# Attention value products half a chunk earlier, the convolution norm's two statistics matmuls one chunk earlier

## The chip, the core and the metric

The kernel runs on one core of one Trainium2 chip. The metric is the device time of one execution in microseconds, the lower the better. Before the change the median of three runs is 650.92 us (650.64 to 651.39).

## What is computed

Two layers of a decoder trunk over 256 positions of 1024 channels. Each layer multiplies its input by one wide matrix (nine blocks of 1024 columns), runs a convolution branch and an attention branch on the results, gates both, merges them and normalizes. Cut to what matters here:

```python
def conformer_conv(a_val, a_glu, conv_w, conv_b, cln_g, cln_b, w_pw2):
    h = a_val * jax.nn.sigmoid(a_glu)
    h = lax.conv_general_dilated(h, conv_w[:, None, :], ...) + conv_b   # depthwise, 31 taps
    h = jax.nn.silu(layer_norm(h, cln_g, cln_b))
    return h @ w_pw2

def hybrid_layer(x, ...):
    u = x @ w_in + b_in
    a_val, a_glu, a_z, q, k, v, b_z, g_a, g_b = jnp.split(u, SPLIT_POINTS, axis=-1)
    h_a = conformer_conv(a_val, a_glu, ...) * jax.nn.silu(a_z)
    y_a = h_a @ w_proj_a
    o = moba_attention(rope(q), rope(k), v)      # 16 heads of 64; causal softmax over 256 positions here
    y_b = (o * jax.nn.silu(b_z)) @ w_proj_b
    merged = jax.nn.sigmoid(g_a) * y_a + jax.nn.sigmoid(g_b) * y_b
    return layer_norm(DEEPNORM_ALPHA * x + merged @ w_out, ln_g, ln_b)
```

## The kernel before

**Chunks.** Every weight matrix is cut into blocks of 256 columns. A block is loaded as float32 (`raw`), and ScalarE (ACT) copies it to a rounded part `hi` in four pieces (L120) while GpSimd (POOL) subtracts to get the rest, `lo` (L124). `gemm_a` (L154) multiplies one block in two chunks, c = 0 and 1, of 128 output channels each. A chunk is 16 matmuls on TensorE (PE): seven `hi` matmuls of 512 columns (L176), eight `lo` matmuls of 256 (L174), and a last `hi`. Its result `mm` lies in one of three PSUM buffers; ACT copies the low half out (`lw`, L182 or L184) and VectorE (DVE) adds it to the high half (L187).

**The stages of a layer.** Value rows first, then the blocks of `A_GLU`, `A_VAL` and `B_Z`, then the 32 chunks of `MID` (Q, K, G_A for each j, then G_B) with the attention between them, then the 8 chunks of `A_Z`, the 8 of `PB` (attention's projection), the 8 of `PW2` (the convolution's), `PA` and `WO`. The convolution's 31 taps run on DVE (L381) in the background until the end of `MID`.

**The attention between chunks.** Eight pairs of heads a layer. A table, `plan`, says after which chunk, or in the middle of which, a pair's three steps are written: `hook(c - 0.5)` is called in a chunk after its eighth matmul, `hook(c)` at its end. `L1`, `L2`, `L3` are the distances in chunks from the pair's K chunk:

```python
at = 2 * n + 1
for p in (2 * j, 2 * j + 1):
    for d, f in ((L1, att_scores), (L2, att_trans), (L3, att_av)):
        plan.setdefault(at + d, []).append((f, p))
    at += 3
```

`att_scores` writes the scores (PE L451), mask and two maxima (DVE L457 to L459), exponentials (ACT L461 twice, L464 twice, each followed by the read of its sum), the reciprocal (DVE L466) and the scaled probabilities `p` (ACT L468, L469, twice). `att_trans` writes six transposes of `p` into two PSUM tiles, `ta` and `tb` (PE L477 to L479), and copies them out as `pa` and `pb` (ACT L482, L483). `att_av` writes the products with the values into the free half of `tb` (PE L491, L494), gates them there (DVE L496) and splits them (ACT L497, DVE L498). The pool of `ta` and `tb` has two buffers, so the `tb` of a pair waits until L498 of the pair before has read its own. Pairs are three chunks apart, and a pair's transposes stand in the same chunk as the scores of the next pair.

**The convolution's norm.** `cln_mu` is the mean's matmul (PE L542) with subtraction and squares, called at the end of `A_Z` chunk `CM`; `cln_var` is the variance's matmul (PE L551) with the chain to the reciprocal root, called after `PB` chunk `CV`; `CB` says after which `PB` chunk each of the eight `cln_b` stands, which write the two halves of `hc` that `PW2` multiplies.

**What sets the order.** On PE the order inside one block of weights is as written; the next block's matmuls may be put between. On ACT and DVE a scheduler decides when the program is built: the order of each engine's instructions is fixed then, and each engine runs its own in that order.

Of the kernel before, what the change touches and what calls it, by code (L numbers as in the profile page):

```python
# [31 lines left out]
NEG = -1e30  # L32
EARLY = 6
NH2 = 2
CM = 5.0
CV = 1
CB = [[], [], [0, 1], [2, 3], [4, 5], [6, 7], [], []]
KE = 7
KN = 5
L1, L2, L3 = 2.5, 5.5, 7.0  # L40
MAN = ''
WARM = 34
NA = 4
# [27 lines left out]
def decoder_trunk(ctx: ExitStack, tc: tile.TileContext, a, out):  # L71
# [19 lines left out]
    def u_pair(name):  # L91

        both = pair.tile([P, KT, 2, S], F32R, tag="p", name=name)
        return both[:, :, 0, :], both[:, :, 1, :], both
# [51 lines left out]
    def background(n):  # L146
        with tc.high_priority(offset=-LATE):
            for _ in range(min(n, len(conv_ops))):
                conv_ops.pop(0)()
# [153 lines left out]
    for l in range(DEPTH):  # L303
# [244 lines left out]
        def cln_var():  # L548
            f = fold(cln["sq"], cln["sq"])
            vp = cvp.tile([P, 2, S], F32, tag="cv", name=f"cvar{l}")  # L550
            nc.tensor.matmul(vp[:, 0, :], ones, f, start=True, stop=True)  # L551
            u = tmp.tile([P, S], F32, tag="g", bufs=2, name=f"cu{l}")
            y = vp[:, 1, :]
            nc.scalar.activation(u, vp[:, 0, :], AF.Sqrt, bias=eps)
            nc.vector.reciprocal(y, u)
            nc.scalar.activation(u, y, AF.Square)
            nc.vector.tensor_scalar(vp[:, 0, :], vp[:, 0, :], EPS, None, op0=ALU.add)
            nc.vector.scalar_tensor_tensor(u, u, -0.5, vp[:, 0, :], op0=ALU.mult, op1=ALU.mult)
            nc.vector.scalar_tensor_tensor(y, u, 1.5, y, op0=ALU.add, op1=ALU.mult)
            cln["r"] = y  # L560

        def cln_b(ct):
            z = ptp.tile([P, 512], F32, tag="pt", name=f"z{l}_{ct}")[:, :S]
            nc.vector.tensor_tensor(z, cv[:, ct, :], cln["r"], op=ALU.mult)
            nc.scalar.activation(z, z, AF.Silu, bias=pc[:, C_LB + ct : C_LB + ct + 1],  # L565
                                 scale=pc[:, C_LG + ct : C_LG + ct + 1])
            nc.scalar.activation(hc[0][:, ct, :], z, AF.Copy)
            nc.vector.tensor_tensor(hc[1][:, ct, :], z, hc[0][:, ct, :].bitcast(F32), op=ALU.subtract)

        def ev_pb(ct, o):  # L570
            nc.vector.scalar_tensor_tensor(gb[:, ct, :], gb[:, ct, :], 1.0, o, op0=ALU.add, op1=ALU.mult)  # L571
            if ct == CV:
                hc.extend(u_pair(f"hc{l}"))
                cln_var()
            for q in CB[ct]:
                cln_b(q)

        def hook_az(c, j):
            if 2 * j + c == CM:
                background(len(conv_ops))  # L580
                cln_mu()
# [178 lines left out]
```

## Time and profile before

| | us |
|---|---|
| median of three runs | 650.92 |
| the profiled execution, its own time | 650.96 |
| its span, first to last instruction | 649.2 |
| PE busy in the span | 634.4 |
| DVE busy | 486.2 |
| ACT busy | 437.7 |
| POOL busy | 486.2 |

The span leaves 1.76 us of the execution's own time outside. Busy times of PE are modelled ends of pipelined matmuls, so distances from start to start say more than durations.

### The profile page before, as it was taken

To read this page: it belongs to the slowest core of one execution; us is meant where nothing else is said; L and a number is where in the kernel's file an instruction comes from. 1 tells how busy PE (TensorE), PEld (TensorE's weight loads), DVE (VectorE), ACT (ScalarE), POOL (GpSimd) and SP (SyncE) were. 2 spreads that over 40 slices of the span, in tenths; PEclk is the share of its full clock that TensorE was granted. 3 is DMA by queue.
4 is the path that set the end of the run, shared out by engine and by line. 5 is a ranking of instruction groups with operands and counts; after the bars stand their busy time and mean duration, and the time that the engine had idled before them with its cause. 6 is when DMAs were issued, how large, how long until landed. Compare 5 with 4: busy or idle time off the path is not lost.

```text
span 649.2 us, 10602 instructions
## 1 busy us (share of the span) xinstructions
PE 634.4 (98%) x3662; PEld 542.3 (84%) x3662; DVE 486.2 (75%) x1130; ACT 437.7 (67%) x1017; POOL 486.2 (75%) x385
## 2 busy tenths in 40 slices
PE   8999999999999999999999999999999999999995
PEld 6888888887878888988788888888877888889884
DVE  4668989999998666455840999899999886664556
ACT  4775665887778689656527566668777787885640
POOL 0089999777566898989628999996677589999850
PEclk9999999999999999999999999999999999999999
DMA  8975555444333564554653555554433344555401
GB/s 268 349 276 211 194 196 195 159 166 131 131 129 131 195 250 152 201 184 187 259 195 113 212 195 199 192 193 152 174 131 130 130 147 178 195 190 186 174 36 65
DMA packets 19190, 116.06 MB, mean 179 GB/s; under 512 B 2112, under 2 KB 3392, under 8 KB 6208
## 3 DMA queue, kind: packets, MB, share of 16 engines
q1 hardware_dynamic: 18560, 114.85, 48.9%
q8 instruction: 29, 0.48, 0.3%
q10 hardware_dynamic: 576, 0.52, 0.3%
q14 instruction: 25, 0.20, 0.1%
HBM read 114.32 MB, written 1.05 MB: 178 GB/s over the span
## 4 chain that ended last, share of the span: by engine, by line
PE 85%; ACT 7%; DVE 4%; DMA 2%; POOL 1%; issue 1%; ACTq 0%; DVEq 0%
PE mm L176 43%; PE mm L174 23%; PE wo L210 3%; PE v L210 3%; PE v L340 3%; ACT hi L120 3%; PE s L451 2%; PE mm L171 2%; DMA raw<-w 2%; PE tb L491 1%; POOL lo L124 1%; ACT z L565 1%; PE tb L479 1%; PE v L331 1%; PE wps L248 1%
## 5 line engine op out<-in xcount | busy, mean ns | idle before, releaser
L124 POOL TENSOR_TENSOR lo<-raw,hi 128x512 fp32r<-128x512 f32 x380 | 485.8, 1315 | 138.7 <-ACT hi L120 134.2
L176 PE MATMUL mm<-x,hi 128*128 128x512 f32 x1024 | 263.8, 395 | 0.0
L120 ACT ACTIVATE hi<-raw 128x512 fp32r<-128x512 f32 x412 | 235.7, 630 | 21.9 <-DMA raw<-w 15.8
L176 PEld LDWEIGHTS mm<-x,hi 128*128 128x128 f32 x1024 | 183.9, 189 | 34.6 <-issue 2.4
L381 DVE SCALAR_TENSOR_TENSOR cv<-h,pc,cv 128x256 f32<-128x256 f32 x464 | 196.4, 481 | 0.2
L174 PEld LDWEIGHTS mm<-x,lo 128*128 128x128 f32 x1024 | 139.4, 190 | 11.3
L174 PE MATMUL mm<-x,lo 128*128 128x256 f32 x1024 | 147.5, 284 | 0.0
L187 DVE TENSOR_TENSOR mm<-mm,lw 128x256 f32<-128x256 f32 x172 | 73.5, 430 | 81.1 <-ACT lw L182 52.1
L182 ACT ACTIVATE lw<-mm,pc 128x256 f32<-128x256 f32 x128 | 61.4, 480 | 88.3 <-PE mm L176 87.9
L176 PE MATMUL mm<-og,hi 128*128 128x512 f32 x128 | 33.1, 395 | 0.0
L210 PE MATMUL wo<-hi,mg 128*128 128x512 f32 (+1 forms) x144 | 32.6, 367 | 0.2 <-DVE mg L610 0.2
L176 PE MATMUL mm<-ah,hi 128*128 128x512 f32 x128 | 32.4, 392 | 0.0
L124 DVE TENSOR_TENSOR lo<-raw,hi 128x512 fp32r<-128x512 f32 x32 | 25.5, 840 | 6.8 <-ACT hi L120 6.7
L210 PEld LDWEIGHTS wo<-hi,mg 128*128 128x128 f32 x144 | 25.2, 189 | 5.3 <-DVE mg L610 0.9
L184 ACT ACTIVATE lw<-mm 128x256 f32<-128x256 f32 x44 | 16.8, 386 | 16.7 <-PE mm L176 15.8
L176 PEld LDWEIGHTS mm<-og,hi 128*128 128x128 f32 x128 | 23.3, 189 | 4.1
L176 PEld LDWEIGHTS mm<-ah,hi 128*128 128x128 f32 x128 | 23.0, 189 | 4.0
L176 PE MATMUL mm<-hc,hi 128*128 128x512 f32 x96 | 25.1, 396 | 0.5 <-DVE gb L571 0.5
L176 PEld LDWEIGHTS mm<-hc,hi 128*128 128x128 f32 x96 | 17.2, 189 | 4.7 <-ACT z L565 1.3
L174 PEld LDWEIGHTS mm<-og,lo 128*128 128x128 f32 x128 | 17.5, 190 | 1.2
L174 PEld LDWEIGHTS mm<-ah,lo 128*128 128x128 f32 x128 | 17.5, 190 | 1.2
L461 ACT ACTIVATE s<-s,nm 128x256 f32<-128x256 f32 x32 | 14.1, 441 | 5.9 <-DVE nm L459 5.9
(134 smaller groups left out, 710.4 us busy)
## 6 DMA issues: line engine op xcount, KB each, us to landing
raw<-w SPq DMA_DIRECT2D x101, 1024.0 KB, 4.8
raw<-w SPq DMA_DIRECT2D x8, 256.0 KB, 5.2
rows<-pr SPq DMA_DIRECT2D x4, 512.0 KB, 6.2
raw<-w SPq DMA_DIRECT2D x2, 512.0 KB, 7.8
xs<-x SPq DMA_DIRECT2D x1, 1024.0 KB, 7.0
out<-xs SPq DMA_DIRECT2D x3, 256.0 KB, 2.0
xf<-xT ACTq DMA_DIRECT2D x4, 128.0 KB, 5.7
xf<-xT SPq DMA_DIRECT2D x2, 256.0 KB, 4.4
```

The source lines that it names most:

```text
L120: nc.scalar.activation(hi[:, ks, :], raw[:, ks, :], AF.Copy)
L124: eng.tensor_tensor(lo[:, ks, :], raw[:, ks, :], hi[:, ks, :].bitcast(F32), op=ALU.subtract)
L171: nc.tensor.matmul(ps[:, 0, :], (wl if q == 2 else wh)[:, k, cs], both[:, k, int(q == 1), :], start=(n == 0), stop=(n == len(seq) - 1))
L174: nc.tensor.matmul(ps[:, 0, :], wl[:, k, cs], both[:, k, 0, :], start=False, stop=False)
L176: nc.tensor.matmul(ps, wh[:, k, cs], both[:, k, :, :], start=(n == 0), stop=(k == KT - 1))
L182: nc.scalar.activation(t, low, AF.Identity, bias=pcs[0][:, b * KT + ct : b * KT + ct + 1])
L184: nc.scalar.activation(t, low, AF.Copy)
L187: nc.vector.tensor_tensor(kept[:, c if b in (Q, K) else 0, :], o, t, op=ALU.add)
L210: nc.tensor.matmul(o, (xl if q == 1 else xh)[:, kk, ts], (wl if q == 2 else wh)[:, k, cols], start=(kk == 0 and n == 0), stop=(kh == 1 and ...
L340: nc.tensor.matmul(o[t], (xl if r == 1 else xh)[:, kk, ts], (wl if r == 2 else wh)[:, k, :], start=(kk == 0 and r == 0), stop=(kk == 7 and ...
L381: r = nc.vector.scalar_tensor_tensor(dst, src, w, acc[:, c, :], op0=ALU.mult, op1=ALU.add)
L461: nc.scalar.activation(s1[:, e, :], s1[:, e, :], AF.Exp, bias=nm[:, 2 + e : 3 + e], accum_out=sm[:, 2 + e : 3 + e])
```

## The change

Four constants differ. `L3` goes from 7.0 to 6.5: the value products of a pair come one chunk after its transposes in place of one and a half, so they stand in the middle of a chunk (after its eighth matmul) and no longer at its end. `CM` goes from 5 to 4 and `CV` from 1 to 0: the two statistics' matmuls stand one chunk earlier. `CB` moves the eight `cln_b` up by one chunk with them. Nothing is added or removed.

```diff
-CM = 5.0
-CV = 1
-CB = [[], [], [0, 1], [2, 3], [4, 5], [6, 7], [], []]
+CM = 4.0
+CV = 0
+CB = [[], [0, 1], [2, 3], [4, 5], [6, 7], [], [], []]
 KE = 7
 KN = 5
-L1, L2, L3 = 2.5, 5.5, 7.0
+L1, L2, L3 = 2.5, 5.5, 6.5
```

The first place is PE's order in layer 0 around the value products of pair 3 (`tb_3`; `mm_1_1959` is the chunk that they stand at), as a difference:

```order
 L176 MATMUL mm_1_1959<-x_94,hi_1712 128x512 x7
-L174 MATMUL mm_1_1959<-x_94,lo_1713 128x256 x8
-L176 MATMUL mm_1_1959<-x_94,hi_1712 128x512
+L174 MATMUL mm_1_1959<-x_94,lo_1713 128x256
 L491 MATMUL tb_3_1911<-pa_3_1918,v_183 64x256 x2
 L494 MATMUL tb_3_1911<-pb_3_1919,v_183 64x128 x2
+L174 MATMUL mm_1_1959<-x_94,lo_1713 128x256 x7
+L176 MATMUL mm_1_1959<-x_94,hi_1712 128x512
```

Seven `lo` matmuls and one `hi` that stood ahead of the products now stand behind them; the other pairs move alike.

The second place is ACT's order in layer 0 around the softmax of pair 5 (`s0_5`, `p0_0_5` and `p1_0_5`); `lw28_0` and `lw28_1` are the copies out of chunks `mm28_0` and `mm28_1`, `tb0_4` is pair 4's. Before:

```order
L461 ACTIVATE s0_5_2057,sm0_5_2063<-s0_5_2057,nm0_5_2062 128x256
L182 ACTIVATE lw28_0_2133<-mm28_0_2116,pc0_181 128x256
L464 ACTIVATE s0_5_2057,sm0_5_2063<-s0_5_2057,nm0_5_2062 128x128 x2
L468 ACTIVATE p0_0_5_2066<-s0_5_2057,rc0_5_2064 128x128
L469 ACTIVATE p1_0_5_2065<-s0_5_2057,rc0_5_2064 128x256
```

And with the change, from `lw28_0` on:

```order
L182 ACTIVATE lw28_0_2140<-mm28_0_2116,pc0_181 128x256
L461 ACTIVATE s0_5_2057,sm0_5_2063<-s0_5_2057,nm0_5_2062 128x256
L182 ACTIVATE lw28_1_2165<-mm28_1_2148,pc0_181 128x256
L461 ACTIVATE s0_5_2057,sm0_5_2063<-s0_5_2057,nm0_5_2062 128x256
L120 ACTIVATE hi30_2178<-raw30_2104 128x512
L464 ACTIVATE s0_5_2057,sm0_5_2063<-s0_5_2057,nm0_5_2062 128x128
L497 ACTIVATE og0_1120<-tb0_4_2046 128x256
L464 ACTIVATE s0_5_2057,sm0_5_2063<-s0_5_2057,nm0_5_2062 128x128
L502 ACTIVATE ga0_1118<-mm28_0_2116 128x256
L120 ACTIVATE hi30_2178<-raw30_2104 128x512
L468 ACTIVATE p0_0_5_2066<-s0_5_2057,rc0_5_2064 128x128
L469 ACTIVATE p1_0_5_2065<-s0_5_2057,rc0_5_2064 128x256
```

The second exponential of pair 5 stood ahead of both copies out and now stands behind both; a copy L497 of pair 4, a gate L502 and two weight pieces L120 have come in ahead of `p`.

The third place is ACT's order around the softmax of pair 4 (`s_4`, `p_0_4`), where `lw_1` is the copy out of the chunk `mm_1_1959` of the first place. Before:

```order
L461 ACTIVATE s_4_1922,sm_4_1928<-s_4_1922,nm_4_1927 128x256
L182 ACTIVATE lw_1_1976<-mm_1_1959,pc_181 128x256
L461 ACTIVATE s_4_1922,sm_4_1928<-s_4_1922,nm_4_1927 128x256
L120 ACTIVATE hi_2002<-raw_1889 128x512
L464 ACTIVATE s_4_1922,sm_4_1928<-s_4_1922,nm_4_1927 128x128
L120 ACTIVATE hi_2002<-raw_1889 128x512
L464 ACTIVATE s_4_1922,sm_4_1928<-s_4_1922,nm_4_1927 128x128
L120 ACTIVATE hi_2002<-raw_1889 128x512 x2
L468 ACTIVATE p_0_4_1931<-s_4_1922,rc_4_1929 128x128
```

And with the change:

```order
L182 ACTIVATE lw_1_1983<-mm_1_1959,pc_181 128x256
L120 ACTIVATE hi_2002<-raw_1889 128x512
L461 ACTIVATE s_4_1922,sm_4_1928<-s_4_1922,nm_4_1927 128x256
L497 ACTIVATE og_1120<-tb_3_1911 128x256
L461 ACTIVATE s_4_1922,sm_4_1928<-s_4_1922,nm_4_1927 128x256
L120 ACTIVATE hi_2002<-raw_1889 128x512
L464 ACTIVATE s_4_1922,sm_4_1928<-s_4_1922,nm_4_1927 128x128
L120 ACTIVATE hi_2002<-raw_1889 128x512
L464 ACTIVATE s_4_1922,sm_4_1928<-s_4_1922,nm_4_1927 128x128
L120 ACTIVATE hi_2002<-raw_1889 128x512
L468 ACTIVATE p_0_4_1931<-s_4_1922,rc_4_1929 128x128
```

The first exponential has gone behind the copy out, and L497 of pair 3, which stood behind `p`, has come between the two. Layer 1 has the same orders at all three places.

## Rows read from the trace of the kernel before

**Rows 1.** The page, busy us by engine (share of the span), instructions

```profile
PE 634.4 (98%) x3662; PEld 542.3 (84%) x3662; DVE 486.2 (75%) x1130; ACT 437.7 (67%) x1017; POOL 486.2 (75%) x385
```

**Rows 2.** Stretch of layer 0's attention: length, busy by engine (instructions), clock, DMA

```profile
113.00:214.00 101.00, 99.43 (x619) 82.41 (x619) 93.00 (x227) 79.74 (x221) 70.72 (x57) 1.00 0.41 144
```

**Rows 3.** Waits of PE: for whom, us in total, times, longest

```profile
PE tb L479 <- DVE og L498: 3.1, 4, 0.8
```

**Rows 4.** Timeline of PE, transposes of pair 5: start, us, what [idle before]

```profile
179.26 2.00 PE L176 MATMUL mm<-x,hi 128*128 128x512 f32 x8
...
181.22 0.27 PE L477 MATMUL ta<-ident,p 128*128 128x128 f32 x1
181.33 0.27 PE L478 MATMUL ta<-ident,p 128*128 128x128 f32 x1
182.40 0.30 PE L479 MATMUL tb<-ident,p 128*128 128x128 f32 x1 [0.79 <-DVE og L498]
```

**Rows 5.** Timeline of DVE, pair 5's maxima and rotation, pair 4's split

```profile
174.07 0.43 DVE L187 TENSOR_TENSOR mm<-mm,lw 128x256 f32<-128x256 f32 x1
...
177.56 0.48 DVE L381 SCALAR_TENSOR_TENSOR cv<-h,pc,cv 128x256 f32<-128x256 f32 x1
...
181.84 0.41 DVE L498 TENSOR_TENSOR og<-tb,og 128x256 fp32r<-128x256 f32 x1
```

**Rows 6.** Timeline of PE, a chunk behind scores and one behind value products

```profile
160.65 1.10 PE L174 MATMUL mm<-x,lo 128*128 128x256 f32 x7
161.59 2.00 PE L176 MATMUL mm<-x,hi 128*128 128x512 f32 x8
...
164.38 0.39 PE L176 MATMUL mm<-x,hi 128*128 128x512 f32 x1
...
165.50 1.88 PE L176 MATMUL mm<-x,hi 128*128 128x512 f32 x7
167.22 1.12 PE L174 MATMUL mm<-x,lo 128*128 128x256 f32 x8
```

**Rows 7.** Timeline of ACT, softmax of pair 4 and start of pair 5's `p`

```profile
162.02 0.48 ACT L182 ACTIVATE lw<-mm,pc 128x256 f32<-128x256 f32 x1 [1.32 <-PE mm L176]
...
164.87 0.47 ACT L182 ACTIVATE lw<-mm,pc 128x256 f32<-128x256 f32 x1 [0.33 <-PE mm L176]
165.24 0.44 ACT L461 ACTIVATE s<-s,nm 128x256 f32<-128x256 f32 x1
...
165.69 0.63 ACT L120 ACTIVATE hi<-raw 128x512 fp32r<-128x512 f32 x1
166.21 0.34 ACT L464 ACTIVATE s<-s,nm 128x128 f32<-128x128 f32 x1
...
166.55 0.64 ACT L120 ACTIVATE hi<-raw 128x512 fp32r<-128x512 f32 x1
...
168.46 0.38 ACT L468 ACTIVATE p<-s,rc 128x128 f32<-128x128 f32 x1
168.71 0.49 ACT L469 ACTIVATE p<-s,rc 128x256 f32<-128x256 f32 x1
...
169.67 0.42 ACT L497 ACTIVATE og<-tb 128x256 fp32r<-128x256 f32 x1
169.93 0.52 ACT L182 ACTIVATE lw<-mm,pc 128x256 f32<-128x256 f32 x1
...
178.47 0.37 ACT L468 ACTIVATE p<-s,rc 128x128 f32<-128x128 f32 x1 [0.24 <-DVE rc L466]
```

**Rows 8.** Timeline of ACT, pair 0's last `p`

```profile
124.88 0.50 ACT L469 ACTIVATE p<-s,rc 128x256 f32<-128x256 f32 x1
```

**Rows 9.** Timeline of PE, the transpose that reads it

```profile
125.47 0.29 PE L478 MATMUL ta<-ident,p 128*128 128x128 f32 x1
```

**Rows 10.** Timeline of PE, first two PW2 chunks of layer 0

```profile
255.44 1.54 PE L176 MATMUL mm<-hc,hi 128*128 128x512 f32 x6
...
261.41 2.00 PE L176 MATMUL mm<-hc,hi 128*128 128x512 f32 x8
```

## Prediction

> **What bounds the kernel now.** I read the page's busy times first. PE is busy 98% of the span, VectorE and GpSimd 75%, ScalarE 67% [rows 1]; only PE's own stops, or more work on PE, can change the time much. The table of stretches shows the same where the change acts: of the 101.00 us of layer 0's attention PE is busy 99.43, at a granted clock of 1.00, which is the 2.4 GHz level [rows 2]. So I looked for PE's waits. One kind lies in the attention: a transpose into `tb` that waits for the split L498, four times, 3.1 us in total [rows 3]. The timeline shows what one costs: pair 5's second transpose starts at 181.33, the third not until 182.40, with seven `lo` matmuls behind it that need nothing new [rows 4]. L498 of pair 4 runs from 181.84 to 182.25 [rows 5] and releases it. The loss is the distance less a normal spacing: 1.07 - (181.33 - 181.22) = 0.96 us.
>
> PE's measure elsewhere: a plain chunk lasts 164.38 - 161.59 = 2.79 us [rows 6]. From the start of a chunk's last `hi` to transposes in the middle of the next chunk it is 181.22 - 179.26 = 1.96 us [rows 4], which are eight `hi` and one `lo`. The other seven `lo` are thus 2.79 - 1.96 = 0.83, one `lo` 0.12, one `hi` 0.23.
>
> **What goes away.** First, the four waits for `tb`. The value products move ahead by seven `lo` and a `hi`, 0.83 + 0.23 = 1.06 us, and the scheduler puts L496 to L498 earlier on their engines too: in ACT's new order pair 4's L497 stands ahead of pair 5's `p`, so that bank is read before the transposes can start at all. 4 x 0.96 = 3.84 us. Second, the norm. `PW2` is the only stage that waits for it: its first two chunks take 261.41 - 255.44 = 5.97 us [rows 10] in place of 5.58. With the statistics and `hc` one chunk, 2.79 us, earlier, the 0.39 goes, once a layer: 0.78. The two statistics matmuls cost PE the same at any chunk's end. Their vector work hides behind the `A_Z` and `PB` chunks, where nothing on PE waits for it; without that cover the 0.39 would only stay. Together 4.62 us gone.
>
> **What the moved products cost on PE.** They now interrupt a chunk in the middle. The nearest rows: after scores in mid-chunk the seven `lo` take 161.59 - 160.65 = 0.94 in place of 0.83, so coming back costs 0.11; after value products at a chunk's end the seven `hi` take 167.22 - 165.50 = 1.72 in place of 1.61, 0.11 as well [rows 6]. I take no difference. The bounds are 0.11 less and 0.11 more for each of the 16: 1.76 us either way.
>
> **What is late next.** Moving the products moves L497 and, with it, the order of ACT. ACT works its list in order, so one instruction that waits holds all behind it. I walk ACT's new list from the rows of the old one, by distances from start to start [rows 7]: L182 165.24 - 164.87 = 0.37; L461 with its sum read 0.45; L120 0.52; L464 with its sum read 0.34; L468 0.25; L497 0.26; L469 (169.67 - 168.46)/2 - 0.25 = 0.35. L502, a copy of the same size, is taken as L497. The walk of the old list checks it: from 164.87, with one L182, one L461, two L464 and four L120, comes 168.45, and L468 stands at 168.46. L182 starts 0.43 us after the start of its chunk's last `hi` (161.59 to 162.02) [rows 6, 7]. A transpose starts 0.09 us after the `p` it reads is done (124.88 + 0.50 to 125.47) [rows 8, 9].
>
> *Pair 5.* Today its `p` starts at 178.47 [rows 7] and the transposes at 181.22 [rows 4], with 2.3 us to spare. In the new order its second L461 stands behind the copy out of `mm28_1`, the chunk just ahead of the one that holds the transposes. Count from the start of that chunk's last `hi`: L182 at 0.43; then L182, L461, L120, L464, L497, L464, L502, L120 come to 0.37 + 0.45 + 0.52 + 0.34 + 0.26 + 0.34 + 0.26 + 0.52 = 3.06, so L468 starts at 3.49 and is done at 3.87. The first transpose starts at 3.96; PE is there at 1.96. The second needs L469: 3.74 + 0.49 + 0.09 = 4.32, the third 4.43. The fourth needs the second L468: 4.09 + 0.38 + 0.09 = 4.56; the fifth the second L469: 4.34 + 0.58 = 4.92; the sixth ends its slot at 5.14. Unhindered it would be 1.96 + 6 x 0.11 = 2.62. The loss is 2.52 us. It hangs only on PE's chunk end, so PE can't run away from it. The first L461 must be done by then too, and it waits for L459, which DVE now takes behind the rotation. Counted from the last `hi` two chunks ahead: L182 at 0.43, L187 some 0.5 later, from it to the tap behind the rotation 3.49 (177.56 - 174.07) [rows 5], L461 0.45, together 4.9; the copy out of `mm28_1` stands two chunks on, at 5.58 + 0.43 = 6.0. That leaves 1.1 us for the large maximum L458, which now falls in between.
>
> *Pair 4.* Its L461 now starts behind L182 and one L120, with L497 between. From the last `hi` of `mm_1_1959`: L182 at 0.43; then L182, L120, L461, L497, L461, L120, L464, L120, L464, L120 are 0.37 + 4 x 0.52 + 2 x 0.45 + 0.26 + 2 x 0.34 = 4.29, so L468 starts at 4.72. Transposes could start at 2.79 + 1.96 = 4.75; they start at 4.72 + 0.38 + 0.09 = 5.19, the second at 4.97 + 0.58 = 5.55, the third at 5.66, the fourth at 5.32 + 0.47 = 5.79. Two `hi` of the next block follow (0.46), then the last two, ready, end at 6.58 in place of 4.75 + 0.66 + 0.46 = 5.87. The loss is 0.71 us.
>
> The other six pairs' `p` keep clear of their transposes by the same walk, pair 6 barely.
>
> **The sum.** Twice a layer's 2.52 + 0.71 is +6.46; less 4.62 it is +1.84 us. The profiled execution took 650.96 us (0.04 over the runs' median): 652.80. A measurement of this kernel tells about 0.2%, 1.3 us, from no change.
>
> **The rivals.**
> - *The new waits don't come* (faster). Nothing in this trace waits for `p`, and ACT has a third of its time free. Then all 4.62 us stay: 646.3. It decides at one point: with pair 4's 1.42 taken from 4.62, 3.20 is left for two losses at pair 5, so below 1.60 us there in place of 2.52 the kernel gains. Against it, the order is fixed and the walk is right within 0.01 on the old list.
> - *Only pair 4's wait fails to come*: 652.8 - 1.4 = 651.4. Its first transpose is late by 0.44 alone. The same comes if breaking into a chunk is cheaper, 651.0.
> - *More waits follow.* ACT ends pair 5 with two L120 and a gate still owed, and pair 6 has no slack to lose. One more wait of pair 4's size in each layer, or dearer interruptions: 654.2 to 654.6.
> - *The clock falls.* In this trace the clock stayed at 1.00 over a stretch with stops of 0.96 [rows 2, 4], but none of 2.5 us is there to see. If PE fell to the 1.2 GHz level for one chunk after each of the four new waits, that chunk would last 2.79 us more: 652.8 + 11.2 = 664.0. The Trainium skill (TensorE: Matmul & The Clock Gate, section A second HAM failure mode: psum-queue depth-cycling) says that short stops between groups of matmuls can make the clock swing between its two levels; by that rule this case is what the change buys, and so far the trace doesn't bear it out.
> - *The old waits stay too*, the change not doing what it says: 652.8 + 3.84 = 656.6. Against it, L497's new place.
>
> **How the numbers follow.** The forecast 0.66, no new waits 0.05, pair 4 clear or cheaper interruption 0.14, more waits 0.11, clock 0.02, old waits kept 0.02. The time is the forecast's, 652.8. The range, 651.0 to 654.3, takes in both bounds of the interruption and the cases next to the forecast, and leaves out the other three and a part of the further waits, together about 0.15. Slower by over 0.2% needs 652.2 here: most of the forecast (0.58), further waits, clock and old waits: 0.73. Within: the rest of the forecast and the case beside it, 0.22. Faster: 0.05.
>
> **What would show it.** Right: no PE wait of `tb` for L498; waits of the transposes L477 and L478 for ACT's L468 and L469 in pairs 4 and 5 of both layers, some 2.5 us at pair 5 and 0.7 at pair 4 by start distances; the first two `PW2` chunks in 5.58. Wrong: if pair 5's L468 starts well before 3.49 after that last `hi`, or its first L461 is held by DVE until after the copy out (then the loss is larger), or other pairs wait.

## The result, and the profile after

The changed kernel takes 655.17 us (median of six executions, 654.15 to 656.65), the kernel before beside it 651.27 (650.64 to 651.53): a ratio of 1.0062, 95% interval 1.0053 to 1.0072. In the later runs it came to 1.0065 (1.0053 to 1.0078). It is slower, as forecast, but by 3.9 us where 1.84 were forecast, and outside the range of 651.0 to 654.3. The profiled execution took 655.94 us.

The page's row of busy times answers to [rows 1], its row of granted clocks (40 slices) stands below it:

```profile
PE 638.3 (98%) x3662; PEld 545.1 (83%) x3662; DVE 489.3 (75%) x1130; ACT 439.1 (67%) x1017; POOL 485.1 (74%) x385
...
PEclk9999999999989999999999999999999999999998
```

PE is busy 3.9 us longer with the same 3662 matmuls. So besides waits some matmuls have become slower; one slice of the clock's row, in layer 0's attention, is an 8 (the 8 at the end lies behind PE's last matmul). PE's waits, to be read against [rows 3] (for whom, us in total, times, longest):

```profile
PE ta L477 <- ACT p L468: 4.5, 4, 1.9
```

The waits of `tb` for L498 are gone and four waits of the transposes for `p` have come. PE's timeline at pair 4 and at pair 5 in layer 0 (start, us, what, idle before) shows them; the second piece answers to [rows 4]:

```profile
168.88 0.28 PE L174 MATMUL mm<-x,lo 128*128 128x256 f32 x1
169.50 0.33 PE L477 MATMUL ta<-ident,p 128*128 128x128 f32 x1 [0.34 <-ACT p L468]
...
171.06 0.92 PE L451 MATMUL s<-r,r 64*128 64x256 f32 x8
...
180.82 0.28 PE L174 MATMUL mm<-x,lo 128*128 128x256 f32 x1
183.00 0.33 PE L477 MATMUL ta<-ident,p 128*128 128x128 f32 x1 [1.90 <-ACT p L468]
...
184.36 1.49 PE L451 MATMUL s<-r,r 64*128 64x256 f32 x8
185.78 1.86 PE L174 MATMUL mm<-x,lo 128*128 128x256 f32 x7
187.44 2.25 PE L176 MATMUL mm<-x,hi 128*128 128x512 f32 x8
189.53 0.28 PE L174 MATMUL mm<-x,lo 128*128 128x256 f32 x1
```

From that `lo` to the scores an unhindered pair of the kernel before needs 0.86 us (pair 1, 135.79 to 136.65), and 1.33 with two `hi` between, as at pair 4 (pair 2, 146.87 to 148.20):

```profile
135.79 0.28 PE L174 MATMUL mm<-x,lo 128*128 128x256 f32 x1
...
136.65 0.93 PE L451 MATMUL s<-r,r 64*128 64x256 f32 x8
...
146.87 0.28 PE L174 MATMUL mm<-x,lo 128*128 128x256 f32 x1
...
148.20 0.93 PE L451 MATMUL s<-r,r 64*128 64x256 f32 x8
```

Pair 5 now takes 3.54, a loss of 2.68; pair 4 takes 2.18, a loss of 0.85. ACT's timeline ahead of pair 5's `p` shows why, and answers to [rows 7]:

```profile
179.48 0.48 ACT L182 ACTIVATE lw<-mm,pc 128x256 f32<-128x256 f32 x1 [0.90 <-PE mm L176]
179.85 0.44 ACT L461 ACTIVATE s<-s,nm 128x256 f32<-128x256 f32 x1
...
181.16 0.39 ACT L497 ACTIVATE og<-tb 128x256 fp32r<-128x256 f32 x1
...
182.55 0.40 ACT L468 ACTIVATE p<-s,rc 128x128 f32<-128x128 f32 x1
```

From the copy out L182 to `p` it is 3.07 us, back to back; 3.06 were worked out. At pair 4 the same distance is 4.31 (4.29 worked out).

What was not in the sum stands behind pair 5's stop. PE in stretches (length, busy and instructions, granted clock, DMA share, GB/s):

```profile
180.00:184.30 4.30, 2.32 (x12) 1.00 0.76 244
184.30:187.50 3.20, 3.20 (x18) 0.54 0.00 0
187.50:189.50 2.00, 2.00 (x9) 0.88 0.54 106
189.50:193.50 4.00, 4.00 (x27) 1.00 0.50 209
503.00:507.00 4.00, 3.49 (x19) 0.80 0.24 100
507.00:509.00 2.00, 2.00 (x8) 0.54 0.00 0
```

PE is never idle between 184.30 and 189.50, and yet the clock is near the 1.2 GHz level for some 3 us, in both layers, just behind the stop. Behind pair 4's stop of 0.34 us it stays at 1.00. The eight score matmuls, seven `lo` and eight `hi` take 189.53 - 184.36 = 5.17 us there; at 1.00 the same pieces take 3.63 (an experiment below has them in its rows). The fall costs 1.54 us. In layer 1 the same pieces take 509.93 - 504.79 = 5.14, a cost of 1.51:

```profile
504.79 1.08 PE L451 MATMUL s<-r,r 64*128 64x256 f32 x8
...
509.93 0.28 PE L174 MATMUL mm<-x,lo 128*128 128x256 f32 x1
```

Last, the first two chunks of `PW2`, to be read against [rows 10]:

```profile
258.42 1.77 PE L176 MATMUL mm<-hc,hi 128*128 128x512 f32 x7
...
263.77 0.40 PE L176 MATMUL mm<-hc,hi 128*128 128x512 f32 x1
```

To the last `hi` of the second chunk it is 5.35 us, against 5.97 before: 0.62 gained a layer.

Two ways of reading the traces come back below. One is the time from the scores of pair 0 to the first `PB` chunk, nearly all of the attention, worked out from those two starts in each timeline; before it is 232.66 - 115.35 = 117.31 us in layer 0, and 117.30 in layer 1:

```profile
115.35 0.93 PE L451 MATMUL s<-r,r 64*128 64x256 f32 x8
...
232.66 1.77 PE L176 MATMUL mm<-og,hi 128*128 128x512 f32 x7
```

The other is the mean granted clock of each execution, which every run lists beside its time. It is a rough sign: it takes in the time behind PE's last matmul, where the clock falls too (0.50 from 646.0 us on in the profile of the kernel before), so that profiled executions with no fall before that end have means from 0.995 to 0.998, and one fall of the kind above lowers the mean by under 0.003.

### The profile page after: what moved, and what is told of

The parts are those of the page before. It is cut to its first block, busy times and chain, and to the rows that moved or that the text cites. A ratio compares the mean times of both kernels' runs of the same rounds, so it can differ in the third digit from the quotient of the medians.

```text
span 654.2 us, 10610 instructions
## 1 busy us (share of the span) xinstructions
PE 638.3 (98%) x3662; PEld 545.1 (83%) x3662; DVE 489.3 (75%) x1130; ACT 439.1 (67%) x1017; POOL 485.1 (74%) x385
## 4 chain that ended last, share of the span: by engine, by line
PE 90%; ACT 3%; DMA 2%; DVE 2%; POOL 1%; issue 1%; SPq 0%; DVEq 0%; ACTq 0%
PE mm L176 46%; PE mm L174 26%; PE wo L210 3%; PE v L210 3%; PE v L340 3%; DMA raw<-w 2%; PE s L451 2%; PE mm L171 2%; PE tb L491 1%; ACT hi L120 1%; POOL lo L124 1%; PE ta L478 1%; PE ta L477 1%; PE tb L494 1%; PE tb L479 1%
## 5 line engine op out<-in xcount | busy, mean ns | idle before, releaser
L176 PE MATMUL mm<-x,hi 128*128 128x512 f32 x1024 | 259.8, 394 | 0.0
L120 ACT ACTIVATE hi<-raw 128x512 fp32r<-128x512 f32 x412 | 235.5, 632 | 21.6 <-DMA raw<-w 15.3
L174 PE MATMUL mm<-x,lo 128*128 128x256 f32 x1024 | 153.2, 287 | 0.0
L182 ACT ACTIVATE lw<-mm,pc 128x256 f32<-128x256 f32 x128 | 61.6, 481 | 91.1 <-PE mm L176 90.4
L174 PE MATMUL mm<-og,lo 128*128 128x256 f32 x128 | 17.8, 282 | 0.0
```

Of the source, the lines that this page charges most:

```text
L120: nc.scalar.activation(hi[:, ks, :], raw[:, ks, :], AF.Copy)
L174: nc.tensor.matmul(ps[:, 0, :], wl[:, k, cs], both[:, k, 0, :], start=False, stop=False)
L176: nc.tensor.matmul(ps, wh[:, k, cs], both[:, k, :, :], start=(n == 0), stop=(k == KT - 1))
L182: nc.scalar.activation(t, low, AF.Identity, bias=pcs[0][:, b * KT + ct : b * KT + ct + 1])
```

## The experiments

All were timed against the kernel before on the same chip. The differences in us below are to its median in the same runs, which was 651.1 to 651.5.

### The two parts apart

```diff
 # norm_only: the change with
-L1, L2, L3 = 2.5, 5.5, 6.5
+L1, L2, L3 = 2.5, 5.5, 7.0
 # av_only: the change with
-CM = 4.0
-CV = 0
-CB = [[], [0, 1], [2, 3], [4, 5], [6, 7], [], [], []]
+CM = 5.0
+CV = 1
+CB = [[], [], [0, 1], [2, 3], [4, 5], [6, 7], [], []]
```

> The norm's constants CM, CV and CB as in the change, L3 back at 7.0. Theory: the two parts are independent; the first two chunks of PW2 lose 0.62 us a layer, as the changed kernel's markers show, the four waits of tb for L498 stay, no transpose waits for p: 651.3 - 1.2 = 650.0 us (649.6 to 650.4). Prediction on record: 651.3 - 0.8 = 650.5. Rival: the earlier statistics get in the way of ACT or DVE at the end of the attention, and this part carries some of the loss: 651.3 or more.

> L3 6.5 as in the change, CM, CV and CB back. Theory: this part carries the whole loss, waits of pair 4's and pair 5's transposes for p with the clock's fall behind pair 5's; and the norm's 1.2 us are missing: 655.2 + 1.2 = 656.4 us (655.5 to 657.2). Rival, the loss comes from the norm's part: 650 or less.

The norm alone: 650.59 us, ratio 0.9984 (0.9976 to 0.9993), a gain of 0.9, just above its range of 649.6 to 650.4. `PW2`'s first two chunks take 5.35 in both layers. The attention is as before in layer 0 (117.34); in layer 1 it takes 117.61, and the 0.27 more lies between the scores of pairs 0 and 1, as it does in the profile of the changed kernel. The value products alone: 657.58 us, ratio 1.0090 (1.0077 to 1.0102), a loss of 6.1, above its range of 655.5 to 657.2. So the norm's part gains and the loss is the value products' alone, as the theory had it. The two do not add up to the 3.9 of the change (6.1 - 0.9 = 5.2); how many falls the unprofiled executions had is not known.

The profiled execution of the second gave more than was asked. Its stops at pair 5 are the same 1.90 us in both layers; these are its stretches of PE behind them:

```profile
184.30:187.50 3.20, 3.20 (x22) 1.00 0.00 0
187.50:189.50 2.00, 2.00 (x15) 1.00 0.39 66
503.00:507.00 4.00, 3.96 (x20) 0.64 0.05 18
507.00:509.00 2.00, 2.00 (x10) 0.88 0.29 86
```

In layer 0 the clock did not fall, in layer 1 it did. PE's timeline in layer 0:

```profile
184.65 0.92 PE L451 MATMUL s<-r,r 64*128 64x256 f32 x8
185.50 1.10 PE L174 MATMUL mm<-x,lo 128*128 128x256 f32 x7
186.44 2.00 PE L176 MATMUL mm<-x,hi 128*128 128x512 f32 x8
188.28 0.28 PE L174 MATMUL mm<-x,lo 128*128 128x256 f32 x1
```

188.28 - 184.65 = 3.63, against 5.17 with the fall: this is where the price of 1.54 is from. Its attention takes 118.89 us in layer 0 and 120.46 in layer 1. The waits for `p` alone, at pairs 4 and 5, thus cost 118.89 - 117.31 = 1.58 a layer net of the gone `tb` waits, and the fall comes on top in some executions.

### The changed kernel once more

> The changed kernel once more, unaltered, beside the next kernels. Theory: the clock's fall behind pair 5's stop comes in some executions and in others not, at about 1.5 us each; without one the kernel stands at about before + 2.0 us, with two at + 5.0. The executions spread over some 3 us (before: under 1), and the longer ones show the lower mean clock. Rival: the fall is a fixed part of the stop, the times lie within 1 us of each other, all at + 4 to + 5.

655.34 us (654.78 to 656.15), ratio 1.0065 (1.0053 to 1.0078). The profiled execution, 654.78, has no fall in layer 0 (attention 118.84) and one in layer 1 (120.67). Over both series the eleven executions lie 2.9 to 5.4 above before, at mean clocks of 0.990 to 0.995; the kernel before lies within 1.5 us in each, at 0.995 to 0.998. None of the eleven is near the + 2.0 of a kernel without a fall, so by the times each probably had at least one. The spread in this series alone is 1.4 us, short of the 3 expected, and the order by clock is rough. That the fall comes and goes is shown by the profiles; how often it comes can only be judged from the times.

### PE kept busy through the stop

```diff
-            tb = ptp.tile([P, 4, P], F32, tag="pt", name=f"tb{l}_{p}")
+            tb = ptp.tile([P, 4, P], F32, tag="pt", name=f"tb{l}_{p}"); [nc.tensor.matmul(ta[:, 0, :P], warm, warm, start=True, stop=True) for _ in range({5: 34}.get(p, 0))]
```

> The changed kernel with 34 more matmuls of zeros (128x128, bf16) into ta ahead of pair 5's transposes in both layers, to be overwritten by the transposes; the output stays the same. They need nothing that is late, and fill PE's stop of 1.9 us there. Theory (PE's stop of 1.9 us lets the granted clock fall): p is as late as before, so the stop's 2.7 us a layer stay, but the clock stays at 1.00 behind it and the 1.5 us a layer come back: 655.2 - 3.0 = 652.2 us (651.7 to 653.2, pair 6 may wait some 0.25 us a layer). Rival (the fall has another cause, such as the interrupted chunk or the load of the whole kernel): 655.2 or more, and the same rows of 0.5 to 0.9 granted clock behind pair 5.

654.56 us (654.45 to 655.07), ratio 1.0048 (1.0035 to 1.0060). Its timeline of PE at pair 5 of layer 0, and then the stretches behind it:

```profile
181.78 2.07 PE L475 MATMUL ta<-warm 128*128 128x128 bf16 x34
183.84 0.33 PE L477 MATMUL ta<-ident,p 128*128 128x128 f32 x1
...
185.20 0.92 PE L451 MATMUL s<-r,r 64*128 64x256 f32 x8
186.05 1.10 PE L174 MATMUL mm<-x,lo 128*128 128x256 f32 x7
```

```profile
185.20:188.40 3.20, 3.20 (x23) 1.00 0.00 0
188.40:190.40 2.00, 2.00 (x16) 1.00 0.54 127
```

`p` is as late as before (from the `lo` at 181.66 to the scores it is again 3.54), but PE has no stop and the clock stays at 1.00 in both layers. The other four executions took 0.5 to 0.6 us less than the profiled one, so by the times they had no fall either. So it is the stop that lets the clock fall. The time came out 2.4 us above the 652.2 expected, for two reasons. The 3.0 was taken off the median, as if every execution had two falls. And the new matmuls moved the order again: the attention takes 119.37 and 119.38 us, 0.48 more than with the stop and no fall, all behind pair 5, where pair 6's transposes now wait for `p`. A fall-free kernel of this order would take 651.49 + 2 x (119.37 - 117.31 - 0.62) = 654.4; 654.56 was measured.

### A stop put into the kernel before

```diff
-            nc.vector.reciprocal(rc, sm)
+            [nc.scalar.activation(s1[:, 0, :], s1[:, 0, :], AF.Copy) for _ in range({5: 8}.get(p, 0))]; nc.vector.reciprocal(rc, sm)
```

The second kernel, bact12, has 12 in place of 8.

> The kernel before with eight more copies of pair 5's exponentials onto themselves on ACT (in place, the output stays the same) between the exponentials and the reciprocal, so that p comes some 2.4 us after PE is there; L3 and the norm are as before, no chunk is interrupted by value products. The wait takes the place of the tb wait at pair 5. Theory (a stop alone lets the clock fall): the waits cost 1.7 us a layer net, the clock's fall behind them 1.5 more: 651.3 + 3.4 + 3.0 = 657.7 us (656.7 to 659.0), granted clock below 1.00 behind pair 5 in both layers. Rival (the stop costs its own length only): 651.3 + 3.4 = 654.7 (653.9 to 655.5), clock at 1.00.

> The kernel before with twelve copies in place of eight ahead of pair 5's p, so that PE's stop there is some 5 us in place of 2.5. Asks whether the clock's fall depends on the stop's length. Theory (the longer the stop, the surer the fall): every execution shows it, in both layers, at 1.0 to 1.5 us each; before + 8.7 + 2 to 3 = 662 us, mean clock 0.993 or less in all. Rival (the fall comes and goes whatever the length): times in two or three groups between before + 8.7 = 660 and 663, some with a mean clock of 0.997.

With eight copies: 655.25 us, +3.8, ratio 1.0059 (1.0045 to 1.0073). The profiled execution has falls in both layers (first row below, 0.59), and took 656.86 at a mean clock of 0.992. Three others took 655.11 to 655.25 at 0.997 and 0.998, one 655.83 at 0.995. So neither theory had it whole: the stop of 1.91 us, with L3 at 7.0 and no broken chunk, does let the clock fall, but in the profiled execution only, and by time and mean clock perhaps once in one of the other four.

With twelve copies: 663.16 us (662.54 to 664.0), +11.7, ratio 1.0179 (1.0165 to 1.0193), all five at mean clocks of 0.987 to 0.992, as the first theory expected. Its stop is 4.55 us; the clock falls while PE still waits, and stays down longer. PE in stretches, of the first and then of the second kernel:

```profile
183.40:187.60 4.20, 4.20 (x21) 0.59 0.12 49
```

```profile
181.30:185.80 4.50, 0.01 (x1) 0.88 0.52 213
185.80:189.00 3.20, 3.14 (x14) 0.50 0.29 64
189.00:193.00 4.00, 4.00 (x18) 0.68 0.52 211
```

### ACT's order repaired

```diff
-HP = 0
+HP = 20          # hp20: the change; bhp10: the kernel before, with HP = 10
```

`HP` is how far ahead of the rest the attention's steps are put when the orders of ACT and DVE are fixed.

> The changed kernel with the attention's steps given precedence over the rest when the program is built (the constant HP from 0 to 20): ACT's list then has all of pair 5's and pair 4's exponentials and p ahead of the copies out and weight pieces that stood between. Theory (the loss is ACT's order, not the moved products): no transpose waits for p, the clock stays at 1.00, one wait of tb of some 0.5 us a layer is left, the gains stay: before - 4.0 us, a ratio of 0.994 (0.992 to 0.996). Rival (value products in the middle of a chunk cost by themselves): before or slower.

> The kernel before with HP at 10 and nothing else changed: says how much of a gain under HP is HP's alone. Theory: one of the two waits of tb a layer goes and PW2 still waits for the norm: before - 2.6 us, a ratio of 0.996 (0.994 to 0.998), about 1.5 us behind the changed kernel under HP. Rival (precedence itself is worth nothing, the change's earlier products are): before.

The change under HP 20: 651.81 us, ratio 1.0017 (1.0008 to 1.0026). Not the forecast gain, and by the total the rival seemed right. The trace says otherwise. These are the three largest of PE's waits:

```profile
PE cmu L542 <- DVE fold L386: 2.8, 2, 1.4
PE wps L248 <- ACT warm L245: 2.7, 1, 2.7
PE tb L479 <- DVE og L498: 0.9, 2, 0.4
```

No transpose waits for `p` and the clock stays at 1.00 at pair 5. But the mean's matmul, now one chunk earlier, waits 1.42 us a layer for the last fold of the taps, from 223.05 to 224.47 in layer 0. The norm alone has that matmul in the same place and no such wait: PE comes to it at 224.14, and the fold is done at 222.60. So two things used up the slack. PE, which no longer stops, comes 1.1 us sooner; and under HP 20 VectorE ends the fold at 224.41, 1.8 us later (224.61 in the kernel before under HP 10, so precedence does that without the earlier products as well). The two folds, first of the norm alone, then of the change under HP 20:

```profile
220.44 2.16 DVE L386 TENSOR_TENSOR fold<-h,fold 128x256 f32<-128x256 f32 x2
...
221.98 2.43 DVE L386 TENSOR_TENSOR fold<-h,fold 128x256 f32<-128x256 f32 x2
```

The cover that the prediction counted on (vector work behind `A_Z`) is there only while PE is late enough and VectorE early enough.

The kernel before under HP 10: 648.92 us, ratio 0.9965 (0.9951 to 0.9978), on the 0.996 expected. Attention 116.22 us in both layers: one of the two `tb` waits is gone without any earlier products.

### The products one chunk behind for two pairs only

```diff
-                    for d, f in ((L1, att_scores), (L2, att_trans), (L3, att_av)):
+                    for d, f in ((L1, att_scores), (L2, att_trans), (6.5 if p in (2, 4) else 7.0, att_av)):
```

> The changed kernel with the value products one chunk behind only for pairs 2 and 4 of each layer, one and a half for the others; the norm as in the change. Theory: ACT's order around pairs 4 and 5 stays clear of the transposes, no p waits, no fall; the tb wait of one pair stays (0.9 us a layer), the other goes: before - 2.8 us, a ratio of 0.9957 (0.994 to 0.9975). Rival (any pair's product in mid-chunk costs): before or slower.

651.63 us, ratio 1.0004 (0.9996 to 1.0013): no gain. `p` waits for nobody, as expected, but pair 5's `tb` waits for L498 1.73 us in each layer where 0.9 was reckoned:

```profile
180.68 0.33 PE L478 MATMUL ta<-ident,p 128*128 128x128 f32 x1
182.74 0.30 PE L479 MATMUL tb<-ident,p 128*128 128x128 f32 x1 [1.73 <-DVE og L498]
```

So one stop of the kernel before went and the other grew by as much. Counted from the scores of pair 0, L498 starts at the same time (66.54 us, before 66.49), while PE comes to pair 5's transposes 0.98 us sooner (64.89, before 65.87), since it no longer stops at pair 3: the stop has only moved. The clock stayed at 1.00 in the profile, which is one of five executions of 650.76 to 650.89 us. The other six took 651.63 to 653.0, at mean clocks of 0.993 to 0.996; whether the clock fell in them is not shown.

### Both repaired

```diff
-CM = 4.0
+CM = 4.5
-HP = 0
+HP = 20          # hp20_cm45; hp20_cm45_l37 also has L3 = 7.0
```

> The changed kernel with HP 20 and the mean's matmul half a chunk later (CM 4.5 in place of 4.0; CV and CB as in the change). Theory: under HP 20 nothing was lost by the value products; the mean's matmul stood 1.42 us a layer waiting for the last fold of the taps, since PE comes to it earlier while VectorE's taps end at the same time. Half a chunk later it stands clear: the run with CM 4.0 less 2.8 us, a ratio to before of 0.997 (0.993 to 0.9985). Rival (value products in mid-chunk are what costs): no better than with CM 4.0, 1.001 or more.

> The same with L3 back at 7.0: the value products at the chunk's end, so that only precedence and the norm's place differ from the kernel before. Theory: with ACT's order right, half a chunk on the value products is worth next to nothing either way, 0 to 0.7 us slower than with 6.5. Rival (a product that breaks into a chunk costs PE 0.1 us each): 1.8 us faster than with 6.5.

With the products one chunk behind: 648.87 us, ratio 0.9957 (0.9945 to 0.9970). One and a half behind: 647.59 us, ratio 0.9942 (0.9929 to 0.9954). Both beat both kernels, and the wait for the fold is gone. The first bears out the theory, the second falls between theory and rival, and its place settles the matter: the attention takes 116.01 and 116.02 us with the early products, 116.03 in both layers with the late ones. Take off the one `tb` wait that is left (pair 5's scores to pair 6's are 0.69 and 0.67 over the plain 11.08), and both are at 115.3 to 115.4, as is the kernel before without its two waits (117.31 - 2 x 0.96). The 1.3 us between the two kernels lie in layer 0's `WO`, from its first matmul to the transposes behind it (23.60 against 22.37 in the profiles), where the first waits 0.8 us for VectorE's L610, which writes the low part of the merged values. So breaking into a chunk costs nothing that these profiles show (0.04 us a layer at most), and half a chunk's distance is worth nothing once ACT's order is right.

## Why the prediction was wrong, point by point

*The gone waits* (3.84 for four). Right: none is left, and the attention of kernels without them is 117.31 - 115.35 = 1.96 us shorter a layer, 0.98 each.

*The norm* (0.78). The place was right, the size too small: 0.62 a layer, 1.24, as both traces and the run of this part alone show. The 5.97 us that the prediction set against two whole chunks ends at the second chunk's last `hi`, one matmul short; the piece to set it against is 5.35.

*Breaking into a chunk* (nothing, 1.76 either way). Right, 0.0 within some 0.05 over the eight pairs of a layer.

*Pair 5's and pair 4's late `p`* (2.52 and 0.71). Right in cause, place and nearly in size: 2.68 and 0.85. Pair 5's six transposes start 0.06 to 0.15 us after the times of the walk. The walk of ACT's new order was right within 0.02. Net of the gone `tb` waits a layer's attention loses 1.58 where the prediction has 2.52 + 0.71 - 1.92 = 1.31.

*The sum.* Without a fall of the clock it would be 2 x (1.58 - 0.62) = +1.92 us, 652.9 on the profiled 650.96, against 652.80 forecast. The norm's larger gain (0.46 over both layers) and the larger waits (0.60) nearly cancel.

*The rival "the clock falls"*, given 0.02 and left out of the sum, is the step that failed. The clock fell, behind pair 5's stop alone: 1.54 us in layer 0 and 1.51 in layer 1 of the profiled execution, which with the 652.9 makes 655.9 (655.94 measured), and on the median about 3.9 - 1.9 = 2.0 us over the two layers. That rival had all four stops answered and a whole chunk at 1.2 GHz, 2.79 us each. It should have been split: pair 4's stop, shorter than that of [rows 4] which left the clock alone, with little chance, pair 5's with a large one and a price of up to 2.79. "None of 2.5 us is there to see" was a reason for a wide range, and was read as a reason against.

The Trainium skill (TensorE: Matmul & The Clock Gate, section HAM oscillation — how this bites in real kernels) describes a PE whose waits between groups of matmuls send it back to the slow clock each time; it is nearer to this case than the section named in the prediction. The traces agree in kind, with 0.50 to 0.59 behind stops of 1.9 and 4.55 us, though not each time: six of eight stops of 1.9 us were followed by a fall.

## What to carry to other kernels

A wait of PE has a second price in the clock behind it, and that price is uncertain from execution to execution: a stop longer than any in the trace belongs in the sum with a chance, not among the remote rivals. Where a program's orders are fixed at build time, moving one engine's step reorders the others around it, so read the order first and look for the late instruction at the next wait; a part that changes nothing by itself can decide the result by that. And slack between two engines can go from both ends when an order is mended: PE came sooner to the fold, and precedence for the attention made the fold later.

## What the runs showed of the hardware

The granted clock fell behind stops of 1.9 us in some executions and layers and not in others, with the same instructions: of the two stops in each of four profiled executions with such a stop, two, one, one and two were followed by a fall. Behind 4.55 us it fell in both layers of the profile, and all five mean clocks were low. Behind the two stops of 1.73 us (products behind for two pairs) there was none in the one profile, nor behind the two of 1.42 us (the change under HP 20), and behind 0.8 us or less none was seen anywhere. Keeping PE busy with matmuls of zeros through the stop kept the clock up in both layers of the profile. What decides at 1.9 us is open. The Trainium skill (TensorE: Matmul & The Clock Gate, section What's actually happening) says that the watch over PE's activity runs freely and does not start with the kernel, which would allow one stop to be answered differently each time; no run here shows that.
